# Forgetting attention: exponentials ranked behind the outputs of the unit in front, and query evacuations tied behind the emptying of the output tile

## The chip, the core and the metric

The kernel runs on one core of a Trainium2 chip. The metric is the device time of one execution in microseconds (us); the median of several runs is given. The engines are TensorE (PE; its weight loads are shown as PEld), VectorE (DVE), ScalarE (ACT), GpSimd (POOL) and SyncE (SP, which issues the DMAs). Each executes its own instructions in the order in which the program lists them, and they wait for each other through semaphores.

## The reference

A trunk of two layers over a sequence of 1024 tokens with 1024 features, in float32. Layer 0 mixes tokens by softmax attention with forgetting (16 heads of 64), layer 1 by gated linear attention; each is followed by a SwiGLU network, and every sub-layer is RMS-normed and modulated by vectors computed from `c`. The change lies in the attention of layer 0:

```python
q, k, v, f_logit = jnp.split(h @ w_in, [D_MODEL, 2 * D_MODEL, 3 * D_MODEL], axis=-1)   # 16 heads of 64
log_f = jax.nn.log_sigmoid(f_logit + b_f)
cum = jnp.cumsum(log_f, axis=1).transpose(0, 2, 1)
for blk in range(S // Q_BLOCK):                       # 8 blocks of 128 queries
    logits = einsum('bqhd,bkhd->bhqk', q[:, qs:qe], k[:, :qe]) * 64 ** -0.5
    logits = logits + cum[:, :, qs:qe, None] - cum[:, :, None, :qe]
    logits = where(causal, logits, -inf)
    outs.append(einsum('bhqk,bkhd->bqhd', softmax(logits), v[:, :qe]))
return concatenate(outs) @ w_out
```

## The kernel before

Every float32 product is made of three products of a high and a low part (`mm3`, lines 259 to 262: high x high, high x low, low x high), or of two where the parts lie stacked. So each result in PSUM that feeds another product is first split: ScalarE copies the rounded high part, VectorE subtracts it from the value (`split`, line 162).

**A unit of attention** is (p, a, g): pair p of heads (0 to 7), head a of the pair (0 or 1), group g of 256 queries (0 to 3). The groups go in the order 0, 3, 1, 2 (`ORDER`), so that a pair has eight units and attention 64. A unit has two halves in the program.

`scores(u)`: products of queries and keys into a score tile `s_b` (two banks of PSUM), a mask product for the diagonal block (line 1062, or 1048 for even g), then on VectorE `least` (line 1024), which adds the cumulated gates, writes the logits to the SBUF tile `lp_s` and keeps their minimum (the signs are turned). Then `weights` for each of the two query blocks: an exponential on ScalarE with its row sum (line 1031), a reciprocal on VectorE (1032), a scaling on GpSimd (1033).

`outputs(u, lps)`: transposes of the weights on TensorE into `t_b` (line 1085, three banks), their split into `pt_s` (lines 163 and 164), products with v into the output tile `o_b` (lines 1097 and 1099), and the emptying of it: ScalarE copies one half to `ot` (line 1113), VectorE adds the other (1114) into `oT_s`. The output tile has one bank, `orr`, so that a unit's products with v cannot begin before the unit in front has been emptied.

`attention(p)` works one unit behind: it traces the scores of a unit, then the outputs of the unit in front of it (`pending`), then goes on. The unit in front of a pair's first is the last of the pair before.

**Projections between.** While attention works on pair p, the queries and keys of pair p + 1 (`qk_proj`, tiles `qk_b`) and part of the v of later pairs (`v_half`, tiles `vps_b`) are projected, in the order queries (two halves of 512 tokens), v, keys. All these tiles come from one ring of two banks, `pj`, as do the small tiles `mp_b` of the modulation sums. A query half is 24 products of 512 columns; its evacuation `q_evac` is four instructions, two on ScalarE (lines 715 and 716, tiles `QA` and `QB`) and two subtractions on VectorE (717 and 719). The evacuated queries go where older queries and keys lay (`qk_tiles`), which must have been read for the last time.

**What sets the order.** `weave` traces attention and projections as two generators, each of which yields its cost on TensorE; the next step is taken from the one that is behind, by totals of 23.0 for a pair's attention and 31.0 for its projections (20.8 for pair 6, which has no v). `LAGS = dict(P=18)` keeps TensorE's instructions of a projection step behind those of the attention step 18 steps back. The traced order is not the issued order: a planner walks through the program with estimated times and writes each engine's list; among instructions that are ready it takes the one traced first. `tc.issue_after(i)` (and `tied(...)`, line 264, for several) puts what is traced inside it behind instruction `i` in the list of `i`'s engine; it binds order alone. `last_of("A")` and `last_of("D")` are the last instructions traced on ScalarE and on VectorE.

Of the kernel before, what the change touches and what calls it, by code (L numbers as in the profile page):

```python
# [9 lines left out]
F32 = mybir.dt.float32  # L10
# [4 lines left out]
ALU = mybir.AluOpType  # L15
# [3 lines left out]
D = 1024  # L19
# [35 lines left out]
def trunk(ctx, tc, x, c, ada_w, ada_b, norm1_g, norm2_g, ffn_w_in, ffn_w_out,  # L55
          fox_w_in, fox_b_f, fox_w_out, gla_w_in, gla_w_a2, gla_b_a, gla_g_o,
          gla_w_out, final_g, out, dbg=None, stop=None):
    nc = tc.nc
# [42 lines left out]
    def hsl(hf):  # L101

        if hf < 2:
            return slice(hf * HALF, (hf + 1) * HALF)
        return slice(hf * 256, (hf + 1) * 256)
# [4 lines left out]
    def psl(t, n=1):  # L110
        return slice(t * P, (t + n) * P)
# [50 lines left out]
    def split(hi, lo, src):  # L162
        nc.scalar.copy(hi, src)  # L163
        nc.vector.tensor_sub(lo, src, hi.bitcast(F32))  # L164
# [99 lines left out]
    def tied(*ins):  # L264

        es = ExitStack()
        for i in ins:
            es.enter_context(tc.issue_after(i))
        return es
# [121 lines left out]
    def last_of(e, n=0):  # L391
        return [i for i in nc.cur_bb.bb.instructions[-400:] if i.engine == ENG[e]][-1 - n]
# [302 lines left out]
    SC = -(64 ** -0.5)  # L695
# [3 lines left out]
    def qk_tiles(p):  # L699
# [9 lines left out]
        qk_at[p] = at  # L709
        return {nm: big.tile([P, S], FR, tag=sl, name=f"{nm}{p}") for nm, sl in at.items()}  # L710

    def q_evac(ps, t, hf):
        cs = hsl(hf)
        QA, QB = t["QA"], t["QB"]
        nc.scalar.mul(QA[0:64, cs], ps[0:64, :], SC)
        nc.scalar.mul(QB[64:128, cs], ps[64:128, :], SC)
        nc.vector.scalar_tensor_tensor(QA[64:128, cs], ps[0:64, :], SC, QA[0:64, cs].bitcast(F32),
                                       op0=ALU.mult, op1=ALU.subtract)
        nc.vector.scalar_tensor_tensor(QB[0:64, cs], ps[64:128, :], SC, QB[64:128, cs].bitcast(F32),
                                       op0=ALU.mult, op1=ALU.subtract)  # L720

    def k_evac(ps, t, hf):
        cs = hsl(hf)
# [279 lines left out]
    def scores(u):  # L1003

        p, a, g = u
        t = qkt[p]
        Qs, K1, KL = (t["QA"], t["KA"], t["KLA"]) if a == 0 else (t["QB"], t["KB"], t["KLB"])
        cm = cums[2 * p + a]
        if g < 2:
            both = lpr([P, (4 * g + 3) * P], F32, f"lp{p}{a}{g}")  # L1010
            lps = [both[:, 0:(2 * g + 1) * P], both[:, (2 * g + 1) * P:]]
        else:
            lps = [lpr([P, (2 * g + 1 + i) * P], F32, f"lp{p}{a}{g}{i}") for i in range(2)]
        st = sm.tile([P, 2, 4], F32, tag="st", bufs=4, name=f"st{p}{a}{g}")
        mcur, seen = [3e38, 3e38], [0, 0]

        def score(ps, qi, k0, k1, start=True, stop=False):
            qs = psl(2 * g + qi)
            nc.tensor.matmul(ps, Qs[:, qs], K1[:, k0:k1], start=start, stop=False)  # L1019
            nc.tensor.matmul(ps, Qs[:, qs], KL[:, k0:k1], start=False, stop=stop)  # L1020

        def least(ps, qi, k0, k1):
            mnew = st[:, qi, seen[qi]:seen[qi] + 1]
            nc.vector.tensor_tensor_reduce(lps[qi][:, k0:k1], ps, cm[:, k0:k1], 1.0, mcur[qi],  # L1024
                                           ALU.add, ALU.min, mnew)
            mcur[qi] = mnew
            seen[qi] += 1

        def weights(qi):
            lp = lps[qi]  # L1030
            nc.scalar.activation(lp, lp, AF.Exp, bias=mcur[qi], scale=-1.0, accum_out=st[:, qi, 2:3])  # L1031
            nc.vector.reciprocal(st[:, qi, 3:4], st[:, qi, 2:3])  # L1032
            nc.gpsimd.tensor_scalar(lp, lp, st[:, qi, 3:4], 1.0, op0=ALU.mult, op1=ALU.mult)  # L1033

        if g % 2 == 0:
            last = [(2 * g + qi + 1) * P for qi in range(2)]
            first = [max(0, w - 256) for w in last]
            for qi in range(2):
                if first[qi]:
                    ps = sr([P, first[qi]], F32, f"s{p}{a}{g}{qi}")  # L1040
                    score(ps, qi, 0, first[qi], stop=True)
                    least(ps, qi, 0, first[qi])
                    yield 0.00085 * first[qi]
            ps = sr([P, 2, 256], F32, f"s{p}{a}{g}")
            views = [ps[:, qi, 256 - (last[qi] - first[qi]):] for qi in range(2)]
            for qi in range(2):
                score(views[qi], qi, first[qi], last[qi], start=qi == 0)
            nc.tensor.matmul(ps[:, :, P:], identr, maskr, start=False, stop=True)
            for qi in range(2):
                least(views[qi], qi, first[qi], last[qi])  # L1050
                weights(qi)
            yield 0.44
        else:
            for qi in range(2):
                Wd = (2 * g + qi + 1) * P
                cuts = (0, Wd) if Wd <= HALF else (0, HALF, Wd)
                for k0, k1 in zip(cuts, cuts[1:]):
                    ps = sr([P, k1 - k0], F32, f"s{p}{a}{2 * g + qi}{k0}")
                    diag = k1 == Wd
                    score(ps, qi, k0, k1, stop=not diag)  # L1060
                    if diag:
                        nc.tensor.matmul(ps[:, k1 - k0 - P:], identr, maskr[:, 0:P], start=False, stop=True)
                    least(ps, qi, k0, k1)
                    yield 0.00085 * (k1 - k0)
                weights(qi)
        return lps

    def outputs(u, lps):

        p, a, g = u  # L1070
        vh = (p % 2) * 2 + a
        vt = vts[p // 2]
        ops = orr([P, 256], F32, f"o{p}{a}{g}")
        pts = []

        def trans(b):
            tp = tr([P, 4, P], F32, f"t{p}{a}{g}{b}")
            last = b == g
            n = 3 if last else 4
            for jj in range(2):  # L1080
                for qi in range(2):
                    if last and jj == 1 and qi == 0:
                        continue
                    i = 2 if last and jj == 1 else 2 * jj + qi
                    nc.tensor.transpose(tp[:, i, :], lps[qi][:, psl(2 * b + jj)], ident)  # L1085
            pt = ptr([P, 2, 4, P], FR, f"pt{p}{a}{g}{b}")
            split(pt[:, 0, 0:n, :], pt[:, 1, 0:n, :], tp[:, 0:n, :])
            pts.append(pt)

        def pv(b):  # L1090
            last = b == g
            for jj in range(2):
                j = 2 * b + jj
                lv = vt[j // 2][:, j % 2, vh].rearrange("p a d -> p (a d)")
                for hl in range(2):
                    if last and jj == 1:
                        nc.tensor.matmul(ops[:, P:], lv, pts[b][:, hl, 2, :], start=False, stop=hl == 1)
                    else:
                        nc.tensor.matmul(ops, lv, pts[b][:, hl, 2 * jj:2 * jj + 2, :],  # L1099
                                         start=j == 0 and hl == 0, stop=False)  # L1100

        for b in range(g + 1):
            trans(b)
            yield 0.44
            if b > 1:
                pv(b - 2)
                yield 0.44
        for b in range(max(0, g - 1), g + 1):
            yield 0.01
            pv(b)  # L1110
            yield 0.44
        ot = sm.tile([64, 256], F32, tag="t1k", name=f"ot{p}{a}{g}")
        nc.scalar.copy(ot, ops[64:128, :])
        nc.vector.tensor_add(oTs[p][a * 64:(a + 1) * 64, g * 256:(g + 1) * 256], ops[0:64, :], ot)

    ORDER = (0, 3, 1, 2)
    LAGS = dict(P=18)
# [2 lines left out]
    def finish(u, lps):  # L1120
        p, a, g = u
        if (a, g) == (0, ORDER[0]):
            oTs[p] = otr([P, S], F32, f"oT{p}")
        yield from outputs(u, lps)
        if (a, g) == (1, ORDER[-1]) and (p < 7 or "oT" in dbg):
            nc.sync.dma_start(oT_d[p], oTs[p])

    def attention(p):
        for a in range(2):
            for g in ORDER:  # L1130
                u = (p, a, g)
                lps = yield from scores(u)
                if pending[0] is not None:
                    yield from finish(*pending[0])
                pending[0] = (u, lps)
                ada0(0.65)
        if p == 7:
            yield from finish(*pending[0])
# [84 lines left out]
    def fox_tail():  # L1223
# [15 lines left out]
        yield from out_chunk(0, 4, oh, xs, 0, 2, "fo", (0, 1), before=load_xT)  # L1239

    weave(attention(7), 27.0, fox_tail(), 30.0)
    split(oh[7].hi, oh[7].lo, oTs[7])
    dump_d("oT", oT_d)
# [878 lines left out]
    for h in range(4):  # L2122
# [5 lines left out]
        done = set()  # L2128
# [102 lines left out]
```

## Time and profile before

| | |
|---|---|
| median of 3 runs | 2391.68 us (2390.41 to 2392.53) |
| the profiled execution | 2392.61 us |
| its span, from first to last instruction | 2390.9 us |
| granted TensorE clock, mean | 0.996 |
| TensorE busy | 2347.1 us (98%) |
| VectorE, ScalarE, GpSimd busy | 1678.5 us (70%), 1184.9 us (50%), 1205.4 us (50%) |
| exponentials (line 1031) | 128, from 109.7 to 607.0 us, median 782 ns |
| query evacuations on ScalarE (line 715) of the pairs 1 to 7 | 14, from 102.0 to 499.3 us |
| copies of an output tile (line 1113) | 64, from 120.5 to 620.1 us |

A row of a view of waits names the engine and line that waited, what ended the wait, and then the total in us, the times and the longest. A row of a timeline gives start and duration in us, engine, line, operation, output and input with their shapes, and in brackets the idle time in front and what ended it. A row of the view of windows gives the stretch, its length, then for each engine the busy time and in brackets the number of instructions, then the granted clock, the busy share of the DMA engines and GB/s.

### The profile page before, as it was taken

What the parts mean: (1) busy time and instruction counts of PE and PEld (TensorE: products, weight loads), DVE (VectorE), ACT (ScalarE), POOL (GpSimd) and SP (SyncE); (2) the same over time, 40 slices, a digit from 0 to 9 for tenths busy, and PEclk for the clock granted to TensorE, in tenths of its full rate; (3) what the DMA queues carried; (4) which work ended last, traced back from release to release, by engine and by line L of the source; (5) the groups of instructions that cost most, each with busy time, mean ns of one, the idle gap of its engine ahead of it and who ended that gap; (6) DMA issues with size and microseconds to landing.
All of it is one profiled execution on the core that took longest, in us unless ns stands there. A gap on an engine that the chain in (4) does not pass through costs nothing.

```text
span 2390.9 us, 35853 instructions
## 1 busy us (share of the span) xinstructions
PE 2347.1 (98%) x12214; PEld 2006.9 (84%) x12214; DVE 1678.5 (70%) x2805; ACT 1184.9 (50%) x2285; POOL 1205.4 (50%) x1073
## 2 busy tenths in 40 slices
PE   7999999999999999999999999999999999999998
PEld 6888888888888888888888898898888888888878
DVE  6567677776697778775688655345696767675787
ACT  4656656675554444435324766563443334345326
POOL 3334444333347878753363565563345666643262
PEclk9999999999999999999999999999999999999999
DMA  9233233323435555447665244444424434357664
GB/s 275 62 109 106 78 117 98 98 89 115 128 113 186 173 171 171 148 171 266 225 226 182 76 142 124 124 158 140 143 99 151 168 131 138 136 189 259 227 195 147
DMA packets 329407, 361.87 MB, mean 151 GB/s; under 512 B 24508, under 2 KB 253016, under 8 KB 329224
## 3 DMA queue, kind: packets, MB, share of 16 engines
q1 hardware_dynamic: 329032, 359.57, 46.3%
q8 instruction: 96, 1.57, 0.3%
q14 instruction: 87, 0.71, 0.1%
q10 hardware_dynamic: 192, 0.02, 0.0%
HBM read 269.25 MB, written 90.24 MB: 150 GB/s over the span
## 4 chain that ended last, share of the span: by engine, by line
PE 84%; DVE 5%; DMA 3%; ACT 3%; POOL 2%; issue 2%; SPq 1%; DVEq 0%; POOLq 0%; ACTq 0%
PE p_b L262 15%; PE p_b L261 15%; PE p_b L260 15%; PE t_b L1085 2%; PE o_b L1099 2%; PE qk_b L260 2%; PE qk_b L261 2%; PE qk_b L262 2%; PE s_b L1019 1%; PE gr_b L261 1%; PE gr_b L260 1%; PE gr_b L262 1%; PE s_b L1020 1%; PE gv_b L261 1%; PE gv_b L262 1%
## 5 line engine op out<-in xcount | busy, mean ns | idle before, releaser
L164 DVE TENSOR_TENSOR o_s<-xv_s,o_s 128x512 fp32r<-128x512 f32 (+1 forms) x376 | 343.3, 916 | 77.6 <-ACT o_s L163 77.2
L163 ACT CAST o_s<-xv_s 128x512 fp32r<-128x512 f32 (+1 forms) x376 | 218.0, 586 | 321.0 <-PE p_b L262 242.6
L261 PE MATMUL p_b<-B,o_s 128*128 128x512 f32 x576 | 224.2, 389 | 0.0
L262 PE MATMUL p_b<-B,o_s 128*128 128x512 f32 x576 | 223.7, 389 | 0.0
L260 PE MATMUL p_b<-B,o_s 128*128 128x512 f32 x576 | 223.1, 389 | 0.0
L795 POOL TENSOR_TENSOR ex_s<-xv_s,xv_s 128x512 f32<-128x512 f32 (+1 forms) x64 | 89.4, 1397 | 256.9 <-DMA xv_s<-in_ffn_w_in_dram 90.9
L1033 POOL TENSOR_SCALAR lp_s<-lp_s,st 128x128 f32<-128x128 f32 (+7 forms) x128 | 100.8, 796 | 232.2 <-DVE st L1032 226.7
L260 PE MATMUL p_b<-T,o_s 128*128 128x512 f32 x480 | 186.7, 389 | 0.0
L261 PE MATMUL p_b<-T,o_s 128*128 128x512 f32 x480 | 186.7, 389 | 0.0
L262 PE MATMUL p_b<-T,o_s 128*128 128x512 f32 x480 | 180.7, 389 | 0.0
L260 PEld LDWEIGHTS p_b<-B,o_s 128*128 128x128 f32 x576 | 108.1, 188 | 22.5
L261 PEld LDWEIGHTS p_b<-B,o_s 128*128 128x128 f32 x576 | 108.1, 188 | 22.5
L262 PEld LDWEIGHTS p_b<-B,o_s 128*128 128x128 f32 x576 | 108.1, 188 | 22.3
L1031 ACT ACTIVATE lp_s<-lp_s,st 128x128 f32<-128x128 f32 (+7 forms) x128 | 98.9, 774 | 47.8 <-DVE st L1024 47.4
L797 POOL TENSOR_TENSOR xv_s<-ex_s,xv_s 128x512 f32<-128x512 f32 (+1 forms) x64 | 85.9, 1342 | 60.4 <-DVE o_s L164 58.2
L163 ACT CAST pt_s<-t_b 128x512 fp32r<-128x512 f32 (+1 forms) x160 | 80.0, 550 | 66.9 <-PE t_b L1085 65.4
L1452 DVE TENSOR_TENSOR ex_s<-ex_s,p_b 128x512 f32<-128x512 f32 x140 | 93.8, 680 | 24.9 <-PE p_b L262 24.7
L261 PEld LDWEIGHTS p_b<-T,o_s 128*128 128x128 f32 x480 | 90.1, 188 | 18.8
L260 PEld LDWEIGHTS p_b<-T,o_s 128*128 128x128 f32 x480 | 90.1, 188 | 18.7
L164 DVE TENSOR_TENSOR pt_s<-t_b,pt_s 128x512 fp32r<-128x512 f32 (+1 forms) x160 | 96.2, 630 | 13.6 <-ACT pt_s L163 13.1
L209 POOL TENSOR_TENSOR w_l_s<-w__s,w_h_s 128x256 fp32r<-128x256 f32 x120 | 88.3, 768 | 34.7 <-ACT w_h_s L206 31.1
L262 PEld LDWEIGHTS p_b<-T,o_s 128*128 128x128 f32 x480 | 90.1, 188 | 18.6
(2001 smaller groups left out, 7471.1 us busy)
## 6 DMA issues: line engine op xcount, KB each, us to landing
xv_s<-in_ffn_w_in_dram SPq DMA_DIRECT2D x176, 256.0 KB, 3.1
hid_B<-x SPq DMA_DIRECT2D x70, 512.0 KB, 2.7
ad_s<-in_ada_w_dram SPq DMA_DIRECT2D x384, 64.0 KB, 2.0
hid_T<-x SPq DMA_DIRECT2D x36, 512.0 KB, 2.9
xv_s<-in_ffn_w_out_dram SPq DMA_DIRECT2D x96, 192.0 KB, 4.8
ada_s<-in_ada_w_dram SPq DMA_DIRECT2D x128, 128.0 KB, 2.7
xv_s<-in_ffn_w_out_dram SPq DMA_DIRECT2D x40, 256.0 KB, 2.8
T2o<-hid_T SPq DMA_DIRECT2D x18, 512.0 KB, 8.6
```

What stands on the lines that cost most here:

```text
L163: nc.scalar.copy(hi, src)
L164: nc.vector.tensor_sub(lo, src, hi.bitcast(F32))
L209: (nc.gpsimd if i < lo_p else nc.vector).tensor_sub(lo[:, cs], rw[:, cs], hi[:, cs].bitcast(F32))
L260: nc.tensor.matmul(ps, ah, bh, start=start, stop=False)
L261: nc.tensor.matmul(ps, ah, bl, start=False, stop=False)
L262: nc.tensor.matmul(ps, al, bh, start=False, stop=stop)
L795: nc.gpsimd.tensor_add(s1, a21, a22)
L797: nc.gpsimd.tensor_sub(a11, s1, a11)
L1031: nc.scalar.activation(lp, lp, AF.Exp, bias=mcur[qi], scale=-1.0, accum_out=st[:, qi, 2:3])
L1033: nc.gpsimd.tensor_scalar(lp, lp, st[:, qi, 3:4], 1.0, op0=ALU.mult, op1=ALU.mult)
L1085: nc.tensor.transpose(tp[:, i, :], lps[qi][:, psl(2 * b + jj)], ident)
L1452: nc.vector.tensor_add(d, d if src is None else dest(G, src), ps)
```

## The change

`scores` no longer issues the exponentials, reciprocals and scalings itself; it returns `weights`, and `attention` calls it for both query blocks after the outputs of the unit in front. `outputs` notes in the list `done` the copy and the add that empty its output tile. `q_evac` ties its four instructions behind those that `done` holds when it is traced: on ScalarE behind the copy, on VectorE behind the add. `done` is empty for the evacuations of pair 0, which come before attention.

```diff
+    done = []
+
     def q_evac(ps, t, hf):
         cs = hsl(hf)
         QA, QB = t["QA"], t["QB"]
-        nc.scalar.mul(QA[0:64, cs], ps[0:64, :], SC)
...
+        with tied(*done):
+            nc.scalar.mul(QA[0:64, cs], ps[0:64, :], SC)
+            nc.scalar.mul(QB[64:128, cs], ps[64:128, :], SC)
+            nc.vector.scalar_tensor_tensor(QA[64:128, cs], ps[0:64, :], SC, QA[0:64, cs].bitcast(F32),
+                                           op0=ALU.mult, op1=ALU.subtract)
+            nc.vector.scalar_tensor_tensor(QB[0:64, cs], ps[64:128, :], SC, QB[64:128, cs].bitcast(F32),
+                                           op0=ALU.mult, op1=ALU.subtract)
...
             for qi in range(2):
                 least(views[qi], qi, first[qi], last[qi])
-                weights(qi)
             yield 0.44
...
-                weights(qi)
-        return lps
+        return lps, weights
...
         nc.scalar.copy(ot, ops[64:128, :])
         nc.vector.tensor_add(oTs[p][a * 64:(a + 1) * 64, g * 256:(g + 1) * 256], ops[0:64, :], ot)
+        done[:] = last_of("A"), last_of("D")
...
-                lps = yield from scores(u)
+                lps, weights = yield from scores(u)
                 if pending[0] is not None:
                     yield from finish(*pending[0])
+                for qi in range(2):
+                    weights(qi)
                 pending[0] = (u, lps)
```

More of the change, by code (lines that the diff above doesn't have):

```diff
@@ L714, in q_evac @@
         QA, QB = t["QA"], t["QB"]
[L715 to L720, printed above, removed]
+        with tied(*done):
[5 more added lines that the diff above has]
+                                           op0=ALU.mult, op1=ALU.subtract)
     def k_evac(ps, t, hf):
```

## The prediction

> **What bounds the kernel now.** I read the page's first two parts, then the windows of the attention stage, then TensorE's waits in it, then the timeline around one stall.
>
> ```profile
> span 2390.9 us, 35853 instructions
> PE 2347.1 (98%) x12214; PEld 2006.9 (84%) x12214; DVE 1678.5 (70%) x2805; ACT 1184.9 (50%) x2285; POOL 1205.4 (50%) x1073
> PEclk9999999999999999999999999999999999999999
> ```
>
> TensorE is busy 98% of the span; ScalarE, which this change reorders, half of it. So only gaps of TensorE can be won, and only a new gap of TensorE costs anything. The windows name TensorE's busy time first and the granted clock third from the end.
>
> ```profile
> 100.00:622.00 522.00, 507.83 (x3260) 455.44 (x3259) 367.16 (x982) 314.18 (x682) 200.20 (x276) 0.99 0.33 102
> 125.00:160.00 35.00, 32.25 (x193) 28.65 (x192) 24.65 (x67) 16.28 (x36) 13.71 (x19) 0.90 0.45 135
> 245.00:290.00 45.00, 45.00 (x301) 41.25 (x300) 29.16 (x80) 27.91 (x62) 21.20 (x30) 1.00 0.30 95
> 290.00:310.00 20.00, 17.43 (x107) 15.26 (x107) 11.35 (x37) 9.56 (x22) 3.80 (x6) 0.91 0.15 53
> ```
>
> Attention runs from about 100 to 622 us, and in it TensorE is idle 522.0 - 507.8 = 14.2 us. That is all there is to win directly. There is a little more through the clock: at 0.91 over 20 us some 1.8 us are lost, at 0.90 over 35 us 3.5 us. Between the bad places (245 to 290) TensorE has no gap at all, so the stage is a few isolated stalls in a full stream. Who ended them:
>
> ```profile
> engine line waited for: us in total, times, longest us
> PE s_b L1019 <- DVE st L1024: 5.0, 5, 2.7
> PE t_b L1085 <- POOL lp_s L1033: 3.1, 2, 1.5
> PE o_b L1099 <- DVE oT_s L1114: 2.7, 2, 1.4
> PE qk_b L260 <- DVE QB L719: 1.4, 2, 0.7
> PE fo010p_b L260 <- ACT x L1236: 1.2, 1, 1.2
> PE mp_b L446 <- DVE QB L719: 0.7, 1, 0.7
> ```
>
> The o_b row is what the change is about: the next unit's products with v wait for L1114, which empties the one bank that all output tiles share. One of the two, on ScalarE, VectorE and TensorE:
>
> ```profile
> 235.29 0.59 ACT L715 ACTIVATE QA<-qk_b 64x512 fp32r<-64x512 f32 x1 [1.56 <-PE s_b L1020]
> 235.89 0.59 ACT L716 ACTIVATE QB<-qk_b 64x512 fp32r<-64x512 f32 x1
> 236.51 0.83 ACT L1031 ACTIVATE lp_s<-lp_s,st 128x640 f32<-128x640 f32 x1
> ...
> 237.34 0.92 ACT L1031 ACTIVATE lp_s<-lp_s,st 128x768 f32<-128x768 f32 x1
> ...
> 238.26 0.35 ACT L1113 COPY ot<-o_b 64x256 f32<-64x256 f32 x1
> ```
> ```profile
> 236.90 0.68 DVE L717 SCALAR_TENSOR_TENSOR QA<-qk_b,QA 64x512 fp32r<-64x512 f32 x1
> 237.59 0.69 DVE L719 SCALAR_TENSOR_TENSOR QB<-qk_b,QB 64x512 fp32r<-64x512 f32 x1
> ...
> 238.64 0.42 DVE L1114 TENSOR_TENSOR oT_s<-o_b,ot 64x256 f32<-64x256 f32 x1
> ```
> ```profile
> 237.63 0.22 PE L1062 MATMUL s_b<-maskr,identr 128*128 128x128 f32 x1
> 239.11 0.51 PE L1099 MATMUL o_b<-pt_s,v_s 128*128 128x256 f32 x2 [1.26 <-DVE oT_s L1114]
> ```
>
> The two exponentials (0.83 and 0.92 us) stand ahead of the copy L1113 on ScalarE, the two query subtractions (0.68 and 0.69 us) ahead of the add L1114 on VectorE. TensorE idles 1.26 us.
>
> **The change part by part.** No instruction is added or taken away and no DMA is moved; the order that the planner writes for ScalarE, VectorE and GpSimd changes, and with it TensorE's.
>
> *Exponentials behind the outputs.* The 128 exponentials, 128 reciprocals and 128 scalings keep their durations:
>
> ```profile
> L1033 POOL TENSOR_SCALAR lp_s<-lp_s,st 128x128 f32<-128x128 f32 (+7 forms) x128 | 100.8, 796 | 232.2 <-DVE st L1032 226.7
> L1031 ACT ACTIVATE lp_s<-lp_s,st 128x128 f32<-128x128 f32 (+7 forms) x128 | 98.9, 774 | 47.8 <-DVE st L1024 47.4
> ```
>
> Their rank falls below the splits and the emptying of the unit in front. A rank decides only where both are ready, so this bites at places like 236.5 us. Gain: the two o_b stalls, 2.7 us. Cost: an exponential that comes later makes its scaling on GpSimd late, then the transposes: the copy (0.35) and a split or two. It is covered by projection products while these last; without them it is a t_b wait, of which the table has two at 1.5 us each. I take zero, since TensorE is full in between; bounds -1.5 (one such stall gone) and +3.1 (two more).
>
> *Query evacuations behind the emptying.* Here the tie is hard, and what matters is which emptying it names. The two generators advance by their yields, attention 23.0 to projection 31.0. The first query half is traced after 8 x 0.65 = 5.2 of projection, so at 5.2 x 23/31 = 3.9 of attention. In pairs 1 to 5 attention has then passed one scores (0.44) and the previous pair's last outputs (2.66), so that `done` names the previous pair's last unit. The second half falls at 7.7 and names the pair's first unit. In pair 0 (no outputs in front) they name units 1 and 2; in pair 6 (31.0 becomes 20.8) also the first and second.
>
> ```profile
> L715 ACT ACTIVATE QA<-qk_b x14: 586/592/597, 102.0 to 499.3; 64x512 fp32r<-64x512 f32 x14
>   PE s_b L1020: 4.1, 3
> L1113 ACT COPY ot<-o_b x64: 351/369/372, 120.5 to 620.1; 64x256 f32<-64x256 f32 x64
> ```
>
> The first query evacuation runs at 102.0 us, the first emptying, behind which it is to go, at 120.5. So the tie is no nudge: the evacuations move by some 10 to 20 us, past all that stands between. Each holds one of the two banks of `pj`, from which every projection tile comes; until it is done the next but one projection cannot start, and projections are what fills TensorE's time. (Middle pairs are milder: their first half already waits for the last scores of the pair whose tiles it overwrites, the s_b row above.) What this costs, by place, from the projection products that would be missing:
>
> ```profile
> 113.20:120.60 7.40, 4.27 (x27) 3.48 (x27) 0.42 (x1) 0.10 (x1) 1.00 0.50 143
> 242.00:246.80 4.80, 2.97 (x19) 2.42 (x18) 0.00 (x0) 0.00 (x0) 1.00 0.01 3
> ```
> ```profile
> 502.40:509.00 6.60, 5.45 (x21) 3.72 (x21) 0.06 (x1) 0.00 (x0) 1.00 0.44 159
> ```
> ```profile
> 246.80:253.40 6.60, 1.77 (x8) 1.30 (x8) 1.66 (x3) 1.00 0.47 159
> ```
> ```profile
> 246.80:253.40 6.60, 0.95 (x7) 0.78 (x6) 0.42 (x1) 0.72 (x2) 1.00 0.47 159
> ```
>
> These are windows restricted to some instructions, with TensorE's time first: v products (the first two rows), query and key products (the third), and what attention itself does next, scores (the fourth) and products with v (the fifth).
> - Start: 27 v products, 4.27 us of TensorE, cannot run before the first emptying plus about 2.4 us (copy 0.35, add 0.42, two 0.59 evacuations, the last subtraction 0.69, handed over between engines). Attention has little to put there. They then fill the t_b stall of 1.5 us that follows: +2.7, bounds 0 and +4.3.
> - Pairs 1 to 5: the v products of 242.0 to 246.8 move behind the last unit's emptying. Attention's next work, 1.77 of scores and 0.95 of products, 2.7 us, would nearly fill the hole of 2.97, but it is a chain (exponential, scaling, transposes, splits, products, copy), and the products stand at its end. I let the scores and half of the products come forward in time, 2.2 us: 0.8 of gap each, +4.0 in all; bounds 0 and 5 x 2.97 = +14.9.
> - Pair 6: the key projection of 502.4 has to wait for the second unit's emptying, some 7 us later by my estimate: 5.45 us of filling gone. Attention's share there is as in the middle pairs, three quarters: 5.45 x 0.27 = +1.5, bounds 0 and +5.5.
>
> Against that, the evacuations no longer stand in front of reciprocals, copies and adds. The waits by window, 425 to 435 us and 290 to 310 us:
>
> ```profile
> PE t_b L1085 <- POOL lp_s L1033: 1.5, 1, 1.5
> ```
> ```profile
> PE s_b L1019 <- DVE st L1024: 1.9, 2, 1.6
> PE qk_b L260 <- DVE QB L719: 0.7, 1, 0.7
> ```
>
> The first (reciprocals queued behind query subtractions) and the three QB waits (1.4 + 0.7 = 2.1) go, besides the 2.7 of above: -6.3; bounds -2.7 (the emptying alone) and -6.3, since what takes their place is in the three costs. With 0.7 of the 2.6 us of stalls in the second window gone, I take 1.0 of the 1.8 us that the clock loses there; bounds 0 and 1.8.
>
> **The clock.** In 290 to 310 us it fell to 0.91 with no stall longer than 1.6 us. [...]
>
> **Sum.** -6.3 - 1.0 + 2.7 + 4.0 + 1.5 = +0.9 us. The profiled execution took 2392.6 us (span 2390.9 and 1.7 around it), 0.9 above the median of the three runs, 2391.7; on the median the forecast is 2392.5: no change that can be told, 0.2% or 4.8 us being about what a measurement of this kernel tells from none.
>
> **The rivals.**
> *Faster: attention fills the holes.* If the chain of attention comes forward far enough, the three costs are near their lower bounds, and -7.3 remains: 2384.5. For it: ScalarE is half idle, VectorE idle for 30%, and every emptying comes sooner. Against: TensorE's stalls today come just where projection products have run out. If the order on VectorE also shifts so that the 2.7 us s_b stall of 125 to 160 us goes, up to 6 us more go with it and its clock loss; the same could as well arise elsewhere. Faster needs 4.8 of the 7.3.
> *Slower: the held banks starve TensorE.* Place: each pair's turn, between the second query projection and the emptying that the first evacuation waits for. Price: start 2.7 and a clock loss like that of 125 to 160, 3.5; five pairs at 1.9 (halfway from 0.8 to the bound), 9.5; pair 6, 3.0; less 7.3: +11.4, that is 2403. It decides from about 1.6 us of gap per pair, where the sum passes +4.8. For it: the QB waits exist already with the evacuation early. Against: the banks' refill is only shifted, and later there is more left to fill with.
> [...]
> *The order hardly changes.* The exponentials' part may do nothing, since rank matters only in ties, and a moved evacuation may meet an already waiting emptying: 2391.7. It speaks against it that 18 us lie between 102.0 and 120.5.
>
> **How the numbers follow.** No measurable change 0.40 (of which 0.05 for the order that hardly changes), its own range 2387 to 2397; attention fills the holes 0.30; starved 0.30. The range reaches to both rivals' times, 2384 to 2403.
>
> **What would show it.** Right: the o_b waits on L1114 gone, first query evacuation after 120 us, new waits of qk_b or vps_b on QB L719 of up to a microsecond, TensorE's idle time in attention within 5 us of 14.2. Wrong towards slower: TensorE gaps above 1.6 us ahead of vps_b at each pair's turn, PEclk below 0.95 near 115 or at the turns. Wrong towards faster: idle time under 9 us with no new row of over 2 us on QB. Outside attention nothing should move but by a shift.

## The result, and the profile after

The changed kernel takes 2404.6 us (median of five, 2402.5 to 2407.0) against 2392.0 of the kernel before: ratio 1.0054, 95% interval 1.0039 to 1.0069, some 13 us slower. The profiled execution took 2404.5 us. Its page begins:

```profile
span 2402.7 us, 35854 instructions
PE 2353.8 (98%) x12214; PEld 2007.7 (84%) x12214; DVE 1677.3 (70%) x2805; ACT 1186.8 (49%) x2285; POOL 1204.5 (50%) x1073
PEclk9999999999999999999999999999999999999999
```

The span grew by 11.8 us, but TensorE's idle time only from 43.8 to 48.9 us; the same 12,214 products are shown as 6.7 us more busy. The weight loads (PEld) are equal to 0.8 us, and the mean clock, 0.996, is the same. So look at windows that hold the same work. Of the changed kernel, the windows that answer to those of the prediction, and one that holds as many products from 100 us on as its first row did of before (3,260):

```profile
100.00:622.00 522.00, 502.64 (x3194) 445.48 (x3192) 363.54 (x974) 311.88 (x674) 197.84 (x274) 0.99 0.33 101
125.00:160.00 35.00, 29.87 (x199) 27.71 (x198) 24.50 (x71) 15.70 (x37) 10.66 (x16) 0.90 0.41 120
245.00:290.00 45.00, 44.13 (x303) 40.18 (x303) 31.10 (x86) 29.42 (x64) 20.15 (x30) 1.00 0.27 83
290.00:310.00 20.00, 18.64 (x128) 16.52 (x127) 14.56 (x45) 12.30 (x28) 5.13 (x8) 1.00 0.29 80
100.00:634.00 534.00, 514.64 (x3260) 455.87 (x3259) 369.24 (x983) 316.76 (x683) 198.99 (x276) 0.99 0.33 99
```

3,260 products took 522.0 us before and 534.0 us after. The rest of the program is the same, first after, then before:

```profile
634.00:2402.00 1768.00, 1757.50 (x8503) 1480.50 (x8501) 1253.43 (x1702) 815.35 (x1513) 969.07 (x754) 1.00 0.50 165
```
```profile
622.00:2390.00 1768.00, 1757.37 (x8503) 1480.30 (x8502) 1256.77 (x1703) 816.24 (x1514) 968.52 (x754) 1.00 0.50 165
```

So the whole 12.0 us lies in attention: TensorE idles 534.0 - 514.6 = 19.4 us there instead of 14.2, and 6.8 us hide in its "busy" time. The weight loads show the loss whole: their idle time went from 522.0 - 455.4 = 66.6 to 78.1 us, some 11.5 more.

TensorE's waits in attention (95 to 650 us) after:

```profile
engine line waited for: us in total, times, longest us
PE s_b L1022 <- DVE st L1027: 4.8, 11, 0.9
PE vps_b L260 <- DVE QB L722: 4.5, 5, 2.1
PE o_b L1100 <- DVE pt_s L164: 4.0, 1, 4.0
PE t_b L1086 <- POOL lp_s L1036: 3.2, 9, 0.5
PE o_b L1100 <- ACT pt_s L163: 1.0, 1, 1.0
PE o_b L1100 <- DVE oT_s L1115: 0.6, 3, 0.2
PE mp_b L446 <- DVE QB L722: 0.4, 1, 0.4
```

Of the waits of before, the ones for the output bank shrank from 2.7 to 0.6 us and those of query products and modulation sums for QB from 2.1 to 0.4. In their place stand v products that wait for QB (4.5), splits (4.0 and 1.0), and many short waits where there were a few long ones: t_b had two at 1.5 us and now nine of at most 0.5, s_b five and now eleven.

To say where the time went, I use for all kernels one number: the lost time, that is the time elapsed less the usual pitch of every product issued so far (pitches as the traces show them in a full stream: 227 ns for 512 columns, 174 for 384, 119 for 256, 109 for a transpose, 62 to 111 for small ones). Its growth by stage, in us:

| | 110–160 | 160–480 | 480–530 | 530–650 |
|---|---|---|---|---|
| before | 9.0 | 18.5 | 4.1 | 4.9 |
| after | 13.3 | 22.3 | 8.3 | 4.6 |

The start costs 4.3 us more, the middle pairs 3.8, pair 6 4.2. Two executions of the same lists can differ by 2.6 us in such a stage, so the single figures are rough: the first kernel of the next section has the lists of before, and lost 6.4 us in 110–160 (before had 6.8 us at half rate there, a granted clock of 0.50 from 145.0 to 151.8 us).

### The profile page after: what moved, and what is told of

It is laid out like the page before. It is cut to its first block, busy times and chain, and to the rows that moved or that the text cites. A ratio compares the mean times of both kernels' runs of the same rounds, so it can differ in the third digit from the quotient of the medians.

```text
span 2402.7 us, 35854 instructions
## 1 busy us (share of the span) xinstructions
PE 2353.8 (98%) x12214; PEld 2007.7 (84%) x12214; DVE 1677.3 (70%) x2805; ACT 1186.8 (49%) x2285; POOL 1204.5 (50%) x1073
## 4 chain that ended last, share of the span: by engine, by line
PE 82%; DVE 6%; DMA 4%; ACT 2%; issue 2%; POOL 2%; SPq 2%; DVEq 0%; POOLq 0%; ACTq 0%
PE p_b L262 14%; PE p_b L261 14%; PE p_b L260 14%; PE t_b L1086 2%; PE o_b L1100 2%; PE qk_b L260 2%; PE qk_b L261 2%; PE qk_b L262 2%; PE gr_b L261 1%; PE gr_b L260 1%; PE gr_b L262 1%; PE vps_b L260 1%; PE gv_b L261 1%; PE gv_b L262 1%; PE gv_b L260 1%
## 5 line engine op out<-in xcount | busy, mean ns | idle before, releaser
L262 PEld LDWEIGHTS p_b<-B,o_s 128*128 128x128 f32 x576 | 108.1, 188 | 22.3
L1456 DVE TENSOR_TENSOR ex_s<-ex_s,p_b 128x512 f32<-128x512 f32 x140 | 94.1, 681 | 27.5 <-PE p_b L262 27.2
L427 POOL TENSOR_TENSOR ad_s<-ad_s,ad_s 128x512 f32<-128x512 f32 x62 | 88.3, 1425 | 33.7 <-ACT ad_s L425 20.4
```

What stands on the lines that cost most here:

```text
L262: nc.tensor.matmul(ps, al, bh, start=False, stop=stop)
L427: nc.gpsimd.tensor_add(acc, acc, raw)
L1456: nc.vector.tensor_add(d, d if src is None else dest(G, src), ps)
```

## The experiments

All ratios are to the kernel before. "Moved" counts the products, of TensorE's 12,096, that one would have to lift out of the list and set elsewhere to get from the list of before to that of the kernel; the planner writes that list anew for each. The figures with "about" are counted from the order in the traces, which gives 1,090 for the ties alone and 1,075 for the changed kernel.

| kernel | ratio, 95% interval | moved |
|---|---|---|
| exponentials' part alone | 0.9999 [0.9990, 1.0008] | 0 |
| ties alone | 1.0046 [1.0033, 1.0059] | 1,088 |
| both, ties in pairs 2–6 | 1.0058 [1.0044, 1.0072] | 1,081 |
| both, tie two units further back | 1.0045 [1.0033, 1.0058] | about 580 |
| ties alone, pair 1 | 1.0015 [1.0006, 1.0023] | 294 |
| ties alone, pair 7 | 1.0019 [1.0010, 1.0027] | 341 |
| ties alone, pairs 2–6 | 1.0053 [1.0040, 1.0065] | 1,081 |
| exponentials held | 1.0082 [1.0068, 1.0096] | 754 |
| TensorE's list of the ties, no ties | 1.0113 [1.0098, 1.0129] | 1,088 |
| exponentials held, TensorE's list of before | 1.0162 [1.0147, 1.0177] | 0 |
| lag 17 | 1.0061 [1.0048, 1.0074] | 864 |
| lag 19 | 1.0064 [1.0051, 1.0076] | 854 |
| changed, lag 17 | 1.0063 [1.0050, 1.0076] | about 1,200 |
| changed, lag 19 | 1.0076 [1.0062, 1.0090] | about 1,060 |

**Which part.** The first kernel takes the change without the ties (`with tied():` in the place of `with tied(*done):`), the second the ties without moving the calls of `weights`.

> Exponentials behind the outputs as in the changed kernel, query evacuations free as before. Theory held banks (the ties hold both banks of pj and starve TensorE): the first query evacuation is back near 102 us, no vps_b waits on QB, and the time is that of before within 3 us (2389 to 2395). Theory late exponentials (scaling and transposes come late, as nine t_b waits of the changed kernel suggest): most of the 12.6 us stay, 2398 to 2405, with five or more t_b waits on lp_s L1036.

> Ties as in the changed kernel, exponentials where they were before. Held banks: nearly the whole loss is here, 2400 to 2407, with vps_b waits on QB. Late exponentials: 2391 to 2396.

Without the ties, moving the exponentials does nothing at all: each engine's list is, instruction for instruction, that of before, and the waits stand where they stood. Of that kernel:

```profile
PE t_b L1086 <- POOL lp_s L1036: 3.1, 2, 1.6
PE o_b L1100 <- DVE oT_s L1115: 2.6, 2, 1.4
```

The exponentials at 236.5 us were ready before the copy was, so tracing them later doesn't set them behind it. The ties alone carry the loss; what the exponentials' part adds to them (1.0054 against 1.0046) can't be told from nothing.

**How long the bank is held.** The changed kernel with ties in the pairs 2 to 6 alone (`2 <= p <= 6`), and with every tie to an emptying two units older (`done[-3]`), which holds the bank from its last product to the first evacuation for some 1 to 11 us (before: 1 to 8) instead of 7 to 25, one of 1 us apart:

> The changed kernel without the ties for the queries of pairs 1 and 7, where the lost time grew by 4.1 us (up to 160 us) and 4.2 us (480 to 530 us). Held banks: these 8 us come back and the middle's 3.8 stay: 2394 to 2398. Late exponentials: little comes back, 2401 to 2405. If the loss at the start is the modulation sums' load that VectorE waits for at 126 to 129 us, and not the tie, the start keeps its loss: 2399 to 2401.

> The changed kernel, but each query evacuation is tied to the emptying two units further back than the last traced one: the one that it ran into at 238 us. Held banks: the bank is held for 3 to 5 us in place of 10 to 20, the o_b waits on the add go, and the time is 2385 to 2393. Late exponentials: 2396 to 2403.

Held banks missed both. The first kernel, 2406.7 us, lies in no theory's range: it no longer loses at the start (8.9 us of lost time in 110–160) nor in 480–530 (4.6), but loses 25.8 instead of the changed kernel's 22.3 in 160–480, and 11.6 instead of 4.6 in 530–650, where it has no tie. The second, 2402.7 us, lies where late exponentials had it, a theory that the exponentials' part alone had ruled out. It has no loss at the start (7.7), where there is no emptying that old to tie to, and its o_b waits are gone (0.4 us in all), but it is as slow as with the long hold. At the turn where before had its 1.26 us wait for the output bank, TensorE's timeline now shows a longer one for the scaling on GpSimd (and another of 1.95 us at 372.7, where before had its other o_b wait):

```profile
240.88 1.09 PE L1086 MATMUL t_b<-identr,lp_s 128*128 128x128 f32 x8 [1.95 <-POOL lp_s L1036]
```

The trace of before shows why. TensorE, then GpSimd, at the stall that the prediction showed:

```profile
239.11 0.97 PE L1099 MATMUL o_b<-pt_s,v_s 128*128 128x256 f32 x6 [1.26 <-DVE oT_s L1114]
...
240.10 1.17 PE L1085 MATMUL t_b<-identr,lp_s 128*128 128x128 f32 x9
```
```profile
238.65 1.69 POOL L1033 TENSOR_SCALAR lp_s<-lp_s,st 128x640 f32<-128x640 f32 x2 [10.83 <-DVE st L1032]
```

GpSimd's two scalings of the unit end at 238.65 + 1.69 = 240.34. The transposes that read them begin at 240.10; the first three read only the first scaling, the fourth waits for the second one too and begins at 240.45, so close behind that the stall is nearly all its slack. Had the output bank come free 1.26 us earlier, TensorE would have come to the transposes by 238.9 and stood there for the scaling instead. The other o_b stall is built alike: there the second scaling ends at 369.32, and the fourth transpose begins at 369.37. At these two places the wait is a link of a chain, not a price of its own.

**Banks.** The other way to take the output bank's wait away is a second bank. The rings take all eight banks that `ps_rings` gives out (2 + 3 + 1 + 2), so it comes from the transposes (`ps_rings(2, 2, 1, 2)` is the control, `(2, 2, 2, 2)` the test); with `(2, 2, 1, 3)` the third bank goes to the projections, once in the kernel before and once in the changed one.

> A control for the next three: the kernel before with two banks for the transposes in place of three, the eighth bank left unused. All theories: 2391 to 2399.

> The control with the free bank given to the output tiles, so that no product with v waits for the emptying, whatever the order on ScalarE. Stall theory (the o_b waits of 1.3 us each are time to win, as the prediction had it): 2.7 us or more below the control. Chain theory (the transposes behind those products wait for the scaled exponentials anyway, so that the stall only moves): the o_b waits go, t_b waits on lp_s L1033 of about a microsecond appear at 235 to 243 and 364 to 372 us, and the time is within 1.5 us of the control.

> The control with the free bank given to the projections. Held banks (TensorE stalls where no projection can start because both banks await evacuation): the stalls at the pairs' turns go, 3 to 8 us below the control. If the stalls there come from the late engines and not from missing projection work: within 1.5 us of the control.

> The changed kernel with the same banks as the one before (three for projections, two for transposes). Held banks: with a third bank the ties cost little, within 4 us of that kernel. If the ties cost by the order on ScalarE and VectorE alone: 10 to 13 us above it.

Ratios: control 1.0079 [1.0067, 1.0092], two output banks 1.0121 [1.0106, 1.0137], three projection banks 1.0090 [1.0076, 1.0103], the same with the change 1.0127 [1.0113, 1.0141]. With two transpose banks the kernel is 19 us slower, and TensorE waits for splits. Waits of the control, then of two output banks:

```profile
PE t_b L1085 <- DVE pt_s L164: 6.3, 15, 1.1
PE xrt_b L1235 <- DVE pt_s L164: 4.7, 1, 4.7
```
```profile
PE t_b L1085 <- DVE pt_s L164: 7.9, 17, 1.7
PE qk_b L260 <- DVE KLB L732: 5.9, 7, 2.2
```

With two output banks the waits for the emptying were gone, and the kernel was 10 us slower than its control, where the prediction's step gives 2.7 faster and the chain theory at most 1.5 us either way. A third projection bank gained nothing on the control either, and with it the change still cost 1.0127 - 1.0090, or 9 us. That speaks against two held banks as the whole cause. But all four kernels have lists of their own, which by what follows makes such a comparison weak.

**Where.** The ties alone, each in a part of the pairs.

> The exponentials stay where they were; the ordering of query evacuations behind an emptying is kept for pair 1 alone. Theory A, losses stay where they are made: the changed kernel lost 4.1 us more than the one before up to 160 us and nothing of that comes back, so 2396 us (ratio 1.0017, range 1.001 to 1.0025), and no difference after 160 us. Rival B, the rest of the schedule answers: a late start moves the later products against the turns, so that the later turns differ too and the time ends anywhere from 2392 to 2400. A trace with the start's 4.1 us and more than 2 us of change after 160 us speaks for B.

> The same for pair 7 alone (its query products run in the last turns of pair 6). Theory A: the 4.2 us that the changed kernel lost between 480 and 530 us, so 2396 us (ratio 1.0017). Rival B: the kernel with pairs 2 to 6 alone lost 10.6 us in the stage after 525 us without any order in pair 7, so what the end of attention loses hangs on when the stream arrives there, and pair 7's own order may cost from 0 to 10 us. Nothing before 480 us should change under either.

> The same for pairs 2 to 6 alone, and the exponentials as before (the kernel with both parts in these pairs took 2406.7 us). Theory A: the 3.8 us of the middle and nothing else, 2396 us. Rival B: as that kernel, 2404 to 2407 us, with the loss in the stage after 525 us. If A held for all three, their excesses over the kernel before (4.1 + 4.2 + 3.8) would add to the changed kernel's 12.1; under B they do not add.

Taken singly the parts cost 3.6, 4.5 and 12.7 us, 20.8 together, and all at once 11.0: they don't add. Pair 1 alone behaves as theory A has it (110–160: 13.4 us lost against 9.0; afterwards 28.1 against 27.5), and pair 7 alone doesn't contradict it (480–530: 7.2 against 4.1, in a profiled execution of 2393.9 us; the median is 2397.7). Pairs 2 to 6 lose 7.6 us more than before in 160–480, where their ties are, twice what the changed kernel loses more there, and 5.2 more in 530–650 (10.1 us), where nothing is tied. (Their lists are, instruction for instruction, those of the kernel with both parts in the pairs 2 to 6: one plan under two names.) Their waits in 525 to 600 us, where before had 1.4 us of two:

```profile
PE xrt_b L1242 <- DMA xr_s<-in_x_dram: 2.0, 1, 2.0
PE s_b L1025 <- DVE st L1030: 1.5, 2, 1.2
...
PE o_b L1105 <- DVE oT_s L1120: 0.8, 1, 0.8
```

**Is it the ties at all?** An ordering on ScalarE that holds no bank: each exponential behind the emptying of the unit two in front (`with tied(*done):` around line 1031 of before).

> The kernel before, query evacuations untouched, with every exponential of a unit ordered on ScalarE behind the emptying of the unit two in front, where the part of the change that only moved the exponentials had let the order go. My prediction's step (a stall that goes is a gain): the two waits for the output bank at 237 and 367 us go (1.26 + 1.38 us), 2389.3 us. Rival, links of one chain: the transposes of the unit behind follow the same exponentials through GpSimd's scaling, so waits for the scaled scores of about the same length stand in the place of the two, 2390.5 to 2393.5 us; if exponentials are held at more turns than these two, up to 2 us more.

2413.2 us, 1.0082 [1.0068, 1.0096]: neither theory. The largest wait is that of query and key products for evacuations that nobody tied:

```profile
PE qk_b L260 <- DVE KLB L734: 6.9, 7, 2.0
PE t_b L1088 <- POOL lp_s L1036: 4.0, 7, 1.6
```

That left the lists. The planner fits TensorE's list to each set of orders, and the next runs force it: at the end of the program each product is put behind the one that stands in front of it in a given list.

> No evacuation is held and no exponential moved; TensorE's list alone is forced, instruction by instruction, to the one that the kernel with the ties alone has (1,088 of its 12,096 products stand elsewhere than before). Theory L (the loss is made by TensorE's list, which the planner wrote anew around the ties): as with the ties, ratio 1.004 to 1.006, 2402 to 2406 us. Theory H (the loss is made by the waits of evacuations and of what stands behind them on ScalarE and VectorE): as before, ratio 0.999 to 1.0015, 2391 to 2396 us; the waits of v products for QB (4.5 us in the changed kernel) are gone under both.

> The exponentials ordered behind the emptying two units in front, as in the run that took 2413 us, but TensorE's list forced to that of the kernel before. Theory L: the 19.5 us came from the 754 products that stood elsewhere, so that under 4 us of it stay: 2392 to 2397 us. Theory H: the held exponentials keep their price, 2408 to 2415 us.

Neither theory again: both are slower than the kernels whose halves they combine. Waits of the first, then of the second:

```profile
PE o_b L1099 <- DVE oT_s L1114: 9.8, 6, 2.5
PE t_b L1085 <- POOL lp_s L1033: 9.5, 8, 1.9
```
```profile
PE t_b L1088 <- POOL lp_s L1036: 32.4, 17, 6.4
```

By the order in the traces, the first has TensorE's and GpSimd's lists of the kernel with the ties, and differs from it in the places of 29 of 2,285 instructions on ScalarE and 46 of 2,805 on VectorE, most of them the freed query evacuations; that costs some 16 us, and the o_b waits on the emptying, 0.6 us with the ties, are 9.8. A list of TensorE is good here only with the lists of the other engines that it was made with. Held exponentials under the old list stall TensorE for 32.4 us at the transposes; the list that the planner made for them brought that to 4.0 and still lost 20 us in all. (The ties with TensorE's list of before weren't tried: products that need a held bank stand in it ahead of those whose emptying the bank waits for.)

The last question is whether any other plan costs as much. `LAGS = dict(P=18)` bounds how far the projections run ahead in TensorE's list; a step less or more orders no evacuation or exponential behind anything.

> The kernel before with LAGS = dict(P=17) in the place of 18: a bound of one step on TensorE's list, which neither holds an evacuation nor an exponential, and after which 864 of TensorE's products stand elsewhere. Theory S (the kernel before stands at a sharp optimum of the planner's lists, and any other list of about so many moves costs about as much per moved product as the ties do, 0.010 to 0.013 us by the four kernels with ties): +9 to +11 us, 2401 to 2405 us. Theory L without S (the ties make a bad list, others are as good): 2389 to 2395 us.

> The same with P=19: 854 products stand elsewhere. Theory S: 2401 to 2405 us. Otherwise 2389 to 2395 us. Were one of the two lags slow and the other not, S in this simple form falls, and the time hangs on which products are moved.

> The changed kernel with LAGS = dict(P=17). Theory S (the kernel before stands at a sharp optimum; every other plan near it lies 10 to 15 us above, the change being one of them): the ties have no price of their own beside another plan, 2402 to 2409 us, as the kernel before with this lag (2406.4). Theory O (the ties have a price of their own of some 12 us, and a foreign lag costs its 13.7 us as well): they add up, 2415 to 2420 us.

> The changed kernel with LAGS = dict(P=19). Theory S: 2402 to 2410 us. Theory O: 2416 to 2421 us. Under S one of the two could by luck lie below the changed kernel's 2404.6 us; below the kernel before (2392) neither theory has it.

Both neighbours of the plan of before cost as much: theory S, but not its price per moved product. The kernel before took 2406.4 us with lag 17 and 2407.7 with lag 19, just above the 2405 that S gave and far from the 2395 of the other; the changed kernel, with 2407.0 and 2409.9, fell where S had it. The price per product isn't constant: the held exponentials move fewer products than the ties (754 against 1,088) and cost nearly twice as much. Windows with as nearly as possible the same 3,260 products from 100 us on, in this order: lag 17, lag 19, changed with 17, changed with 19.

```profile
100.00:635.00 535.00, 513.72 (x3263) 458.81 (x3262) 367.22 (x983) 315.66 (x682) 197.16 (x274) 0.98 0.33 99
```
```profile
100.00:639.00 539.00, 516.81 (x3260) 458.93 (x3259) 373.60 (x984) 316.26 (x683) 198.94 (x276) 0.98 0.32 99
```
```profile
100.00:637.00 537.00, 516.47 (x3262) 458.37 (x3261) 368.84 (x985) 316.81 (x684) 197.81 (x276) 0.99 0.33 99
```
```profile
100.00:640.00 540.00, 519.65 (x3256) 459.10 (x3255) 368.81 (x983) 315.22 (x683) 198.67 (x274) 0.98 0.32 98
```

522 us before (520 in the kernel with the same lists), 534 after, 535 to 540 here. At the same lag the ties add nothing that can be told: 1.0063 against 1.0061 at 17, 1.0076 against 1.0064 at 19, with intervals that overlap widely. The places differ, though. Lost time by stage:

| | 110–160 | 160–480 | 480–530 | 530–650 |
|---|---|---|---|---|
| lag 17 | 4.8 | 28.3 | 7.2 | 8.5 |
| changed, lag 17 | 13.1 | 26.5 | 6.4 | 4.8 |
| lag 19 | 7.8 | 30.0 | 4.2 | 11.1 |
| changed, lag 19 | 13.9 | 24.1 | 9.6 | 7.8 |

The start is the one place where the ties cost time under every lag: 4 to 8 us. It is also clear of the difference between executions: the five kernels with ties in pair 1 lost 12.2 to 13.9 us in 110–160, the nine that lack them and have the banks of before and no forced list 4.8 to 9.0. Behind the start they cost 8 us at lag 18, and save 6 at lag 17 and 4 at lag 19, two lags that cost 16 and 18 us there without a tie. The end of attention goes bad without a tie too; lag 17 in 520 to 600 us shows the waits of the kernel with ties in the pairs 2 to 6:

```profile
PE xrt_b L1235 <- DMA xr_s<-in_x_dram: 1.7, 1, 1.7
PE s_b L1019 <- DVE st L1024: 1.3, 1, 1.3
PE o_b L1099 <- DVE oT_s L1114: 0.8, 1, 0.8
```

No kernel here beats the one before. Lag 17 for the pairs up to the first turn alone (4.8 us lost there against 9.0, or 6.4 with the same lists as before) would be the thing to try; it wasn't.

## Why the prediction was wrong

The forecast was no change, 2392.5 us (2391.7 + 0.9 is 2392.6, and 2391.7 - 7.3 is 2384.4; these tenths change nothing), and the time fell beyond its upper end of 2403. Without the clock, the sum has TensorE's idle time grow by 1.9 us. In attention it grew by 5.2, and 6.8 us came on top inside the busy time, for which the sum has no term. The slower rival had the sign and nearly the size (+11.4), but its reason, starved banks, is shown for the start alone; so its number is luck in good part.

- **"-6.3" for stalls that go, the step that failed first.** The o_b and QB waits did go, all but 1.0 us, just as forecast, and nothing was won. The 4.5 us for v products that came were in the costs. But 5.0 us for splits came, for which the sum had nothing, and the t_b waits, of which 1.5 us were to go, became more and shorter with the same sum. The trace of before had it for the o_b stalls: the transposes behind them follow close on the scaling that they read. I priced a stall by its length, without following what stands next behind it.
- **Local costs.** The sum took the plan as fixed and priced three holes. But the ties alone move 1,088 products, and the list of before lies lower than every list near it that was run: two neighbours that tie nothing cost 14 to 15 us. That term, missing from the sum, is as large as the result. The text said that TensorE's list changes and gave it no price. That the changed kernel paid this price, and not one of its own, is argued from the neighbours and not shown.
- **Start, +2.7, bounds 0 and 4.3.** Measured 4.3 (6.9 against the other execution of the same lists). The mechanism is right, but the longer wait is another. Two waits after, on TensorE:

```profile
120.52 0.39 PE L260 MATMUL vps_b<-wv_0h_s,h0h 128*128 128x256 f32 x1 [2.12 <-DVE QB L722]
...
130.93 0.58 PE L1100 MATMUL o_b<-pt_s,v_s 128*128 128x256 f32 x1 [4.01 <-DVE pt_s L164]
```

  The first is the predicted one. The second I had not seen: a split on VectorE stands behind modulation sums that wait for their own DMA:

```profile
128.88 1.28 DVE L438 SCALAR_TENSOR_TENSOR acc_s<-ada_s,cblk,acc_s 128x256 f32<-128x256 f32 x3 [2.46 <-DMA ada_s<-in_ada_w_dram]
130.19 0.69 DVE L164 TENSOR_TENSOR pt_s<-t_b,pt_s 128x512 fp32r<-128x512 f32 x1
```

- **Pairs 1 to 5, +4.0 less 4.9 for the stalls and 1.0 for the clock there, so -1.9.** Measured +3.8. Gaps ahead of v products came at four places, 0.4 to 0.7 us each and 2.3 in all, less than forecast. But all waits in 160–480 sum to 7.3 us, against 6.9 before: most of the loss lies in a longer pitch inside the busy time.
- **Pair 6, +1.5, bounds 0 and 5.5, less 1.4 of QB waits there, so +0.1.** Measured +4.2. With the 1.0 us of QB waits that went, the cost is 5.2, near its upper bound.
- **Clock, -1.0.** That the loss goes with the stalls was my estimate, and no run shows it. The spell at 298 us went, one at 514 us came (granted clock 0.59 over 514.0 to 518.2 us), and in place of the one at 145 us (0.51 over 145 to 152) there is one at 129 (0.51 over 129 to 136): both kernels spend 10.2 us of attention at half rate.
- **Exponentials, 0.** Right in size; but the reason given, that rank bites at 236.5 us, is wrong.
- **What would show it.** The first evacuation after 120 us: 117.8. Idle time within 5 us of 14.2: 19.4, just outside, and blind to the 6.8 us in busy time.

What stays open: which of the moved products make the 12 us, what lengthens the pitch inside the busy time, and whether a list with the ties could be as good as that of before. That the optimum is sharp is shown at two neighbours, not in general.

## What to carry to other kernels

Where a planner writes the lists, price an ordering edit as a new plan, not as local moves: count the instructions that change place, and run neighbours that change the plan without the edit's meaning (here a lag of 17 and 19) before a cause is told. Profile the same lists twice, to see how far a stage differs by itself. A stall that ends on an engine's work is worth winning only up to the next link: look at what the instructions behind it read and when that is ready. And compare stages by windows that hold the same number of products, with the weight loads beside the matmuls.

## What the runs showed of the hardware

In the kernel before, the granted clock fell to 0.50 for 6.8 us from 145.0 us on and for 3.4 us from 298.6 us on; TensorE's longest idle gap in attention was 2.75 us. Windows of before around the two spells:

```profile
145.00:152.00 7.00, 6.35 (x21) 5.23 (x22) 5.30 (x13) 3.64 (x7) 4.00 (x5) 0.51 0.40 114
298.60:302.00 3.40, 3.14 (x7) 2.48 (x8) 0.97 (x6) 0.24 (x2) 2.38 (x4) 0.50 0.63 217
```

The spells began at 145.0 and 298.6 us, inside the last of these gaps. From TensorE's timeline of before:

```profile
145.65 0.80 PE L1019 MATMUL s_b<-KB,QB 128*128 128x512 f32 x1 [2.75 <-DVE st L1024]
```
```profile
296.58 0.47 PE L1019 MATMUL s_b<-KA,QA 128*128 128x512 f32 x1 [1.64 <-DVE st L1024]
...
297.53 0.41 PE L1019 MATMUL s_b<-KA,QA 128*128 128x384 f32 x1 [0.25 <-DVE st L1024]
...
298.86 0.79 PE L260 MATMUL qk_b<-h0h,w_h_s 128*128 128x512 f32 x1 [0.69 <-DVE QB L719]
```

When the rate fell, 2.1 us of the gap of 2.75 us had passed in the first case; in the second TensorE had idled for 1.64 + 0.25 us and the first 0.4 of 0.69, within 3.6 us. What sets a spell off, and what fixes its length, isn't shown. A spell of 3.4 us costs at most 1.7 us, an estimate from the granted 0.50. Nor do the lists fix the clock: eleven executions of the exponentials' part alone, with the lists of before, had mean clocks of 0.995 to 0.997.
